# Sample rows' attention over the cached keys and values: wide instructions in place of 128-column ones, and the weighting moved to ScalarE

## The chip, the core and the metric

The kernel runs on one core of a Trainium2 chip. The metric is the device time of one execution in microseconds. In the profile PE is TensorE (matrix products), PEld its weight loads, DVE is VectorE, ACT is ScalarE, POOL is GpSimd and SP is the engine whose queue issues most DMAs.

## What is computed

One inference step of a two-layer trunk for 256 prompt tokens and 8 sample tokens at once, with a model width of 2048, in float32. Layer 0 is dilated sliding-window attention, layer 1 a state-space layer; each is followed by a gated feed-forward layer with a short convolution. The change lies in layer 0's attention of the eight sample rows:

```python
def attn_sample(h, kv_bufs, w_qkv, w_o):
    q, k, v = qkv_project(h, w_qkv, PAST_LEN + jnp.arange(S))
    for g, (win, dil) in enumerate(DIL_GROUPS):   # (128,1) (512,4) (2048,16)
        k_all = concatenate([kv_bufs[g][:, :, 0], k[:, :, g]], axis=1)
        v_all = concatenate([kv_bufs[g][:, :, 1], v[:, :, g]], axis=1)
        o, lse = dilated_attend(q[:, :, g], k_all, v_all, ...)   # 128 cached keys and the new one
    o = merge_by_denominator(outs, lses)
    return o @ w_o
```

There are 8 heads of 128 channels and 3 groups; in each head and group a sample row scores 128 cached keys, takes a softmax, and sums the 128 cached values with its weights.

## The kernel before

All activations are held with channels on the partitions and the 264 tokens on the free dimension. The weights stream in as chunks of eight 128x128 blocks, loaded by SP's queue into `wraw` (four buffers). Each chunk is split into a high part `whi` by ScalarE (line 162) and a low part `wlo` by VectorE (line 163), in three buffers each, and every block is used by three matmuls (lines 202 to 204): high by high, high by low, low by high. `gemm` walks through the blocks; at the start of each chunk it advances a counter, runs the work that `later(d, ...)` has put off by d chunks (`pump`), and loads and splits chunks up to two ahead (`ensure`). The framework orders each engine's instructions by its own plan, keeping dependences, so put-off work and splits can change places within an engine's queue; each queue then runs in order.

The query, key and value product `w_qkv` (143 chunks) goes head by head: the keys of head h, the queries of head h+1, the values of head h. In its shade runs the attention. For the prompt rows: `prompt_scores` (scores, mask, maxima on VectorE, exponentials on ScalarE, line 660) and `prompt_out` (transposes, copies, products with the values). For the sample rows and one head:

- `sample_q`: the eight queries are spread over 16 partitions each (`qx`); each partition holds eight cached keys of a group in `kc` (128 x 8 x 128). `dots` makes one dot product with an accumulated output per key on VectorE, four to a half chunk of a group (line 497), into `sc`. `sc` goes through DRAM to `ss`, with the eight rows on eight partitions.
- `sample_softmax`: maxima, exponentials and merge weights; the weighted `ss` goes through DRAM (`pd`) back to 128 partitions.
- `sample_out`: the weights come back as `pk`; for each group the eight cached values of a partition in `vc` are multiplied by their weights and added up in `ac` by VectorE (lines 619 and 621); group g one chunk after group g-1. `fin`, three chunks after the last group is begun, adds over partitions with a product by `sel` (line 625) and splits the result, the operand of the output product `w_o`.

`kc` and `vc` share six buffers (`kvc`), a head's three groups at a time. In the chunks of heads 3 to 5 VectorE and GpSimd also work, a few small steps per chunk, on the tables of the later state-space layer (`z_room`, line 912).

Of the kernel before, what the change touches and what calls it, by code (L numbers as in the profile page):

```python
"""One inference step of the dilated-attention / S5 / ConvFFN trunk on one core.

All activations are held transposed: channels on the partitions, the 264 tokens (256 prompt, 8 sample) on
the free dimension.  Weights stream through in blocks of [128 x 128] and are the stationary operand.  A
float32 product is carried by three float32r passes: each operand is split exactly into a high part H
(float32r) and the rest L, and H*H + H*L + L*H is accumulated in PSUM.
"""
# [19 lines left out]
P = 128  # L27
# [39 lines left out]
def order_grouped(mts, nk, first):  # L67
    """(k, m) blocks: the first `first` M-tiles k-outer, the others one after the other."""
    out = [(k, m) for k in range(nk) for m in mts[:first]]
    out += [(k, m) for m in mts[first:] for k in range(nk)]  # L70
    return out


def qkv_mtiles():
    """Keys of a head, the next head's queries, then the head's values."""
    seq = [(0, 0)]
    for h in range(H):
        seq += [(1, h)] + ([(0, h + 1)] if h + 1 < H else []) + [(2, h)]
    return [(which * G + g) * H + h for which, h in seq for g in range(G)]
# [24 lines left out]
class Put:  # L104
    """Notes calls to an engine for later."""
# [8 lines left out]
class Pin:  # L114
    """Calls to an engine that keep their place in its queue."""
# [8 lines left out]
class Kern:  # L124
# [12 lines left out]
    # ---------------------------------------------------------------- work put off by some chunks of weights  # L137
# [10 lines left out]
    # ---------------------------------------------------------------- helpers  # L148
# [16 lines left out]
    def ensure(self, i):  # L165
        """Load and split the weight chunks up to number i of the whole stream."""
# [13 lines left out]
    def gemm(self, name, order, nk, rhs, evac, lag=0):  # L180
        """Accumulate all blocks of `order`; rhs(k) -> (H, L) moving operands; evac(m, psum).
        The first output is taken out of PSUM `lag` chunks late, and at most two per chunk while catching up."""
# [31 lines left out]
    def ready(self, lst, k):  # L214
        """lst[k], running the put-off work until it is there."""
        while k >= len(lst) or lst[k] is None:
            self.pump()
        return lst[k]

    # ---------------------------------------------------------------- norms  # L220
    def rstd_mean(self, parts, warm=0):
        """-1/2 (mean of squares + eps) of every token, tokens on the partitions: [88, 3] in PSUM."""
# [11 lines left out]
    def rstd_root(self, mh):  # L234
        """2/3 of 1/sqrt(-2 mh): the bit-shift estimate, a step of third and a step of second order."""
# [18 lines left out]
    def rstd_spread(self, w):  # L254
        """[88, 3] -> a PSUM tile with 3/2 of every token's value on all partitions."""
# [9 lines left out]
    def warm(self, n):  # L265
        """Keeps the tensor engine's clock up over a wait: n products that nothing reads."""
# [8 lines left out]
    def rstd_soon(self, acc):  # L275
        """Puts 1/rms of the squares in acc off into the coming chunks; returns the tile that will hold it."""
# [13 lines left out]
    def squares(self, st, x):  # L290
        """st: list with the running sum of squares (made here) and the tile still to be added."""
# [10 lines left out]
    def yevac(self, ys, gi):  # L302
        """Takes a sub-layer's output out of PSUM, times the post-norm's gain; sums its squares."""
# [10 lines left out]
    def reload(self, src, wait):  # L314
        """The residual, loaded tile by tile in the coming chunks."""
# [11 lines left out]
    def operand(self, x, gi, k):  # L327
        """H/L parts of x*g (not yet scaled by 1/rms); the L part is returned as a function."""
# [10 lines left out]
    def residual(self, ys, xs, sq, keep, gi):  # L339
        """x += rms_norm(y)*g tile by tile; then the next sub-layer's operand (gain gi), its squares, the store.  # L340
        Returns rhs(k) and the tile for 1/rms."""
# [45 lines left out]
    # ---------------------------------------------------------------- constants  # L387
# [18 lines left out]
    # ---------------------------------------------------------------- attention  # L406
    def attention(self, ap, rhs, rget):
        """Returns the list that will hold the split o^T tiles, one per head."""
# [16 lines left out]
        def both(what, h, fn):  # L425
            """Runs fn when the second of its two conditions is met."""
# [48 lines left out]
    def sample_q(self, ap, st, h, g):  # L475
        """The 8 sample queries, each on 16 partitions; scores of the cached keys, 8 to a partition."""
# [17 lines left out]
        def dots(g, b0):  # L494
            for b in range(b0, b0 + 4):
                j = ap.tile([P, HD], F32, tag="junk", name=self.nm("junk"), bufs=1)
                nc.vector.tensor_tensor_reduce(  # L497
                    j, kcs[g][:, b], qx[:, g * P : (g + 1) * P], 1.0, 0.0, op0=ALU.mult, op1=ALU.add,
                    accum_out=sc[:, g, b : b + 1],
                )  # L500
            if g == G - 1 and b0:
                self.later(1, write)
# [11 lines left out]
        for g in range(G):  # L514
            self.later(1 + 2 * g, lambda g=g: dots(g, 0))
            self.later(2 + 2 * g, lambda g=g: dots(g, 4))

    def sample_new(self, ap, st, h, g):
        """Products of the sample queries with their own new keys."""
# [6 lines left out]
    def sample_softmax(self, ap, st, h):  # L526
        """Softmax weights of the sample queries over the three groups' cached and new keys."""
# [34 lines left out]
    def merge_exp(self, ap, n, tag, mg):  # L562
        """exp(SCALE*(group max - joint max)); mg is [n, groups] or [n, blocks, groups]"""
# [14 lines left out]
    def merge(self, ap, n, tag, e, l, h):  # L578
        """Merge weight of each group over head 0's sum of that group (as the reference divides)."""
# [13 lines left out]
    def sample_out(self, ap, st, h):  # L593
        """Sum of the cached and new values with the softmax weights."""
# [19 lines left out]

        def add(g):
            for e in range(8):
                w = pk[:, g, e : e + 1]
                if g == 0 and e == 0:
                    nc.vector.tensor_scalar(ac, vcs[g][:, e], w, None, op0=ALU.mult)
                else:  # L620
                    nc.vector.scalar_tensor_tensor(ac, vcs[g][:, e], w, ac, op0=ALU.mult, op1=ALU.add)  # L621
# [8 lines left out]
        for g in range(G):  # L630
            self.later(1 + g, lambda g=g: add(g))
        self.later(3 + G, fin)

    def prompt_scores(self, ap, st, h, g):
        """Masked scores of one group and their exponentials (against the group's maximum)."""
# [40 lines left out]
    def prompt_out(self, ap, st, h, os_):  # L676
        """P transposed group by group, and o^T accumulated over the groups."""
# [6 lines left out]
        def tr(g):  # L684
            # column blocks: (keys 0, queries 0), (keys 0, queries 1), (keys 1, queries 1)
# [23 lines left out]
    # ---------------------------------------------------------------- ConvFFN  # L709
    def ffn_prep(self, fp, l):  # L710
        """Convolution weights, and the part of the sample rows' convolution that the stored rows give."""
# [67 lines left out]
    # ---------------------------------------------------------------- S5  # L779
    def s5_setup(self, p):  # L780
        """What the state-space layer needs of every state: decay, phase, powers of a.  SN small steps at a time."""
# [20 lines left out]
        def exp(out, x):  # L802
            """e**x for x clamped to [-87, 88], to float32's accuracy."""
# [629 lines left out]
```

## Time and profile before

| | us |
|---|---|
| median of 3 runs (2555.21 to 2563.43) | 2557.86 |
| span of the profiled execution | 2555.1 |
| TensorE busy (matmuls) | 2469.9 |
| VectorE busy | 1817.1 |
| ScalarE busy | 1159.4 |
| GpSimd busy | 830.0 |
| attention stage beside `w_qkv`, start to the first third of `w_o` | 45 to 560 |

The time of the profiled execution is not listed apart from its span. Busy times are those in which an engine has at least one instruction running; matmuls overlap, so that a busy TensorE is not one at its peak. A windows row gives, for a stretch in us from the start of the span, its length, the busy time of each engine with the number of instructions in brackets, TensorE's granted clock as a share of 2.4 GHz, the DMA engines' busy share and GB/s.

### The profile page before, as it was taken

How to read it: one execution, taken by the hardware profiler on the slowest of the kernel's cores; microseconds unless marked ns; L12 is line 12 of the kernel's file. 1: busy time of each engine (PE TensorE's matmuls, PEld its weight loads, DVE VectorE, ACT ScalarE, POOL GpSimd, SP SyncE). 2: the span in 40 equal slices, each digit the busy share in tenths (PEclk: the TensorE clock that was granted, in tenths of full speed). 3: DMA queues.
4: the chain of work that ended last, by engine and by line, in shares of the span. 5: the costliest groups of instructions: out<-in, count | busy, mean ns of one | idle time of the engine just before them, and what ended most of it. 6: DMA issues, size and time to landing. Idle time of an engine off the chain costs nothing.

```text
span 2555.1 us, 52974 instructions
## 1 busy us (share of the span) xinstructions
PE 2469.9 (97%) x20998; PEld 2440.6 (96%) x20998; DVE 1817.1 (71%) x3490; ACT 1159.4 (45%) x1754; POOL 830.0 (32%) x1153
## 2 busy tenths in 40 slices
PE   8999999999999999999999988999999999999997
PEld 8999998999999999999999988999999999999997
DVE  6787998778988887764445878445977777764444
ACT  5344433445555555443334333444655545543332
POOL 6333347344899990011003465102100000011001
PEclk9999999999999999999999999999999999999999
DMA  7666666666666665566556677555655555566553
GB/s 274 218 234 220 210 216 203 202 213 218 202 217 217 207 217 189 182 205 199 182 181 213 212 248 240 184 181 168 198 180 179 181 181 182 182 205 200 181 182 117
DMA packets 186874, 512.14 MB, mean 200 GB/s; under 512 B 39281, under 2 KB 68993, under 8 KB 186369
## 3 DMA queue, kind: packets, MB, share of 16 engines
q1 hardware_dynamic: 141808, 457.89, 54.2%
q0 software_dynamic: 7968, 26.71, 3.3%
q10 hardware_dynamic: 36848, 24.16, 3.2%
q8 instruction: 164, 2.69, 0.4%
q14 instruction: 86, 0.70, 0.1%
HBM read 469.80 MB, written 38.88 MB: 199 GB/s over the span
## 4 chain that ended last, share of the span: by engine, by line
PE 77%; DVE 11%; issue 4%; DMA 3%; ACT 2%; POOL 1%; ACTq 1%; SPq 0%; DVEq 0%; POOLq 0%
PE ps L202 25%; PE ps L204 25%; PE ps L203 24%; DVE wlo L163 4%; DMA yb<-y 1%; DVE C L744 1%; ACT whi L162 1%; DVE ac L621 1%; DVE act L367 1%; DMA ident<-in_ident 1%; ACTq L945 0%; POOL qkv L449 0%; DMA y<-yb 0%; DVE z_room L912 0%; DVE act L335 0%
## 5 line engine op out<-in xcount | busy, mean ns | idle before, releaser
L204 PE MATMUL ps<-act,wlo 128*128 128x264 f32 x6176 | 1763.6, 286 | 30.2 <-DVE wlo L163 30.0
L202 PE MATMUL ps<-act,whi 128*128 128x264 f32 x6176 | 1771.1, 288 | 10.6 <-ACT whi L162 8.3
L203 PE MATMUL ps<-act,whi 128*128 128x264 f32 x6176 | 1760.3, 285 | 10.0 <-DVE act L335 9.8
L163 DVE TENSOR_TENSOR wlo<-wraw,whi 128x1024 fp32r<-128x1024 f32 (+1 forms) x775 | 994.2, 1283 | 555.7 <-ACT whi L162 554.6
L162 ACT ACTIVATE whi<-wraw 128x1024 fp32r<-128x1024 f32 (+1 forms) x775 | 815.9, 1055 | 1024.7 <-PE ps L203 800.5
L204 PEld LDWEIGHTS ps<-act,wlo 128*128 128x128 f32 x6176 | 1168.7, 189 | 36.9 <-DVE wlo L163 36.8
L202 PEld LDWEIGHTS ps<-act,whi 128*128 128x128 f32 x6176 | 1166.1, 189 | 16.3 <-ACT whi L162 9.1
L203 PEld LDWEIGHTS ps<-act,whi 128*128 128x128 f32 x6176 | 1169.2, 189 | 13.0 <-DVE act L335 12.2
L294 POOL TENSOR_TENSOR acc<-acc,sq 128x264 f32<-128x264 f32 x112 | 111.3, 993 | 672.8 <-ACT sq L300 670.3
L736 POOL COPY ckeep<-U 128x10 f32<-128x10 f32 x172 | 64.4, 375 | 652.5 <-DVE U L735 651.4
L744 DVE SCALAR_TENSOR_TENSOR C<-U,cw,C 128x255 f32<-128x255 f32 (+1 forms) x344 | 187.7, 547 | 0.7 <-ACT C L738 0.7
L735 DVE TENSOR_TENSOR U<-ps,rstd 128x264 f32<-128x264 f32 x172 | 73.2, 430 | 72.2 <-PE ps L204 71.8
L738 ACT ACTIVATE C<-U,cw 128x264 f32<-128x264 f32 x172 | 102.1, 596 | 17.6 <-DVE U L735 13.1
L449 POOL TENSOR_TENSOR qkv<-qkv,cs 32x264 f32<-32x264 f32 x48 | 57.3, 1194 | 148.7 <-DVE sw L443 47.4
L121 POOL TENSOR_TENSOR z_e<-z_pa,z_pb 128x256 f32<-128x256 f32 x64 | 73.1, 1142 | 5.0
L621 DVE SCALAR_TENSOR_TENSOR ac<-vc,pk,ac 128x128 f32<-128x128 f32 x184 | 69.0, 375 | 2.2
L497 DVE CUSTOM_DVE_ANT_0 junk<-kc,qx 128x128 f32<-128x128 f32 x192 | 58.4, 304 | 1.4
L660 ACT ACTIVATE S<-S,nmg 128x128 f32<-128x128 f32 (+1 forms) x48 | 21.5, 447 | 82.0 <-DVE nmg L655 82.0
L451 POOL TENSOR_TENSOR qkv<-qkv,sw 32x264 f32<-32x264 f32 x48 | 56.4, 1176 | 3.4
L121 POOL TENSOR_TENSOR z_pa<-z_bc,z_tab 128x256 f32<-128x256 f32 x64 | 55.9, 874 | 2.4
L121 POOL TENSOR_TENSOR z_pb<-z_bc,z_tab 128x256 f32<-128x256 f32 x64 | 53.6, 838 | 0.0
L749 ACT ACTIVATE C<-C 128x264 f32<-128x264 f32 x86 | 35.7, 415 | 34.1 <-DVE C L744 30.4
(213 smaller groups left out, 1698.5 us busy)
## 6 DMA issues: line engine op xcount, KB each, us to landing
wraw<-in_w_up SPq DMA_DIRECT2D x344, 512.0 KB
wraw<-in_w_down SPq DMA_DIRECT2D x172, 512.0 KB
wraw<-in_w_qkv SPq DMA_DIRECT2D x143, 512.0 KB
wraw<-in_w_glu SPq DMA_DIRECT2D x64, 512.0 KB
wraw<-in_w_in SPq DMA_DIRECT2D x32, 512.0 KB
kc<-in_kc SPq DMA_DIRECT2D x24, 512.0 KB
vc<-in_vc SPq DMA_DIRECT2D x24, 512.0 KB
wraw<-in_w_o SPq DMA_DIRECT2D x16, 512.0 KB
```

Source lines behind the costliest of these rows:

```text
L121: return lambda *a, **k: self.tc.keep_in_program_order(getattr(self.eng, name)(*a, **k))
L162: self.nc.scalar.activation(hi, src, AF.Copy)
L163: self.nc.vector.tensor_tensor(lo, src, hi.bitcast(F32), op=ALU.subtract)
L202: nc.tensor.matmul(o, hi[:, c], xh, start=first, stop=False)
L203: nc.tensor.matmul(o, hi[:, c], xl, start=False, stop=False)
L204: nc.tensor.matmul(o, lo[:, c], xh, start=False, stop=last)
L294: nc.gpsimd.tensor_tensor(st[0], st[0], st[1], op=ALU.add)
L621: nc.vector.scalar_tensor_tensor(ac, vcs[g][:, e], w, ac, op0=ALU.mult, op1=ALU.add)
L735: nc.vector.tensor_tensor(u, ps[:, 0:NT], rget(), op=ALU.mult)
L736: nc.gpsimd.tensor_copy(keep[:, m, :], u[:, NP - 2 : NT])
L738: nc.scalar.activation(c, u, AF.Identity, bias=cw[:, 3, m : m + 1], scale=cw[:, 2, m : m + 1])
L744: nc.vector.scalar_tensor_tensor(c[:, s:NP], u[:, 0 : NP - s], cw[:, j, m : m + 1], c[:, s:NP], op0=ALU.mult, op1=ALU.add)
```

## The change

The dot products of a group become two instructions on VectorE, one chunk apart: `products` multiplies the whole tile of 128x1024 by the query, repeated over the eight keys, in place; `sums` adds up the 128 channels of each of the eight keys. For the values, `weigh` multiplies the eight value blocks of a group in place by their weights on ScalarE, eight instructions of 128x128 with a per-partition scale; a chunk later `add` on VectorE adds group 1's tile, and then group 2's, to group 0's (128x1024 each), and `halve` adds the halves of that tile until 128 columns are left in `ac`. `halve` runs in the chunk of the last `add`, and `fin` is put off by one chunk more than before. The diff also empties comment lines, which leaves most lines where they were.

```diff
-        def dots(g, b0):
-            for b in range(b0, b0 + 4):
-                j = ap.tile([P, HD], F32, tag="junk", name=self.nm("junk"), bufs=1)
-                nc.vector.tensor_tensor_reduce(
-                    j, kcs[g][:, b], qx[:, g * P : (g + 1) * P], 1.0, 0.0, op0=ALU.mult, op1=ALU.add,
-                    accum_out=sc[:, g, b : b + 1],
-                )
-            if g == G - 1 and b0:
+        def products(g):
+            nc.vector.tensor_tensor(
+                kcs[g], kcs[g], qx[:, g * P : (g + 1) * P].unsqueeze(1).to_broadcast([P, 8, HD]), op=ALU.mult
+            )
+
+        def sums(g):
+            nc.vector.tensor_reduce(sc[:, g], kcs[g], axis=AX.X, op=ALU.add)
+            if g == G - 1:
                 self.later(1, write)
...
         for g in range(G):
-            self.later(1 + 2 * g, lambda g=g: dots(g, 0))
-            self.later(2 + 2 * g, lambda g=g: dots(g, 4))
+            self.later(1 + 2 * g, lambda g=g: products(g))
+            self.later(2 + 2 * g, lambda g=g: sums(g))
...
+        def weigh(g):
+            for e in range(8):
+                nc.scalar.activation(vcs[g][:, e], vcs[g][:, e], AF.Copy, scale=pk[:, g, e : e + 1])
+
         def add(g):
-            for e in range(8):
-                w = pk[:, g, e : e + 1]
-                if g == 0 and e == 0:
-                    nc.vector.tensor_scalar(ac, vcs[g][:, e], w, None, op0=ALU.mult)
-                else:
-                    nc.vector.scalar_tensor_tensor(ac, vcs[g][:, e], w, ac, op0=ALU.mult, op1=ALU.add)
+            if g:
+                self.tt(vcs[0], vcs[0], vcs[g], ALU.add)
+
+        def halve():
+            v = vcs[0]
+            self.tt(v[:, 0:4], v[:, 0:4], v[:, 4:8], ALU.add)
+            self.tt(v[:, 0:2], v[:, 0:2], v[:, 2:4], ALU.add)
+            self.tt(ac, v[:, 0], v[:, 1], ALU.add)
...
         for g in range(G):
-            self.later(1 + g, lambda g=g: add(g))
-        self.later(3 + G, fin)
+            self.later(1 + g, lambda g=g: weigh(g))
+            self.later(2 + g, lambda g=g: add(g))
+        self.later(2 + G, halve)
+        self.later(4 + G, fin)
```

## Rows read from the trace of the kernel before

**Rows 1.** The page's shares of the engines: busy us, share, instructions.
```profile
PE 2469.9 (97%) x20998; PEld 2440.6 (96%) x20998; DVE 1817.1 (71%) x3490; ACT 1159.4 (45%) x1754; POOL 830.0 (32%) x1153
```

**Rows 2.** Windows of the attention stage, columns PE, PEld, DVE, ACT, POOL, clock, DMA.
```profile
75.00:100.00 25.00, 23.19 (x186) 22.37 (x184) 24.38 (x117) 11.90 (x24) 4.11 (x7) 1.00 0.70 232
120.00:150.00 30.00, 25.60 (x179) 24.62 (x180) 28.94 (x92) 12.48 (x30) 13.06 (x16) 0.89 0.61 198
260.00:280.00 20.00, 17.89 (x146) 17.46 (x145) 19.61 (x70) 9.38 (x21) 8.28 (x9) 1.00 0.46 143
315.00:420.00 105.00, 95.63 (x748) 92.60 (x747) 103.36 (x352) 41.28 (x79) 57.25 (x70) 0.99 0.60 201
280.00:315.00 35.00, 35.00 (x282) 34.56 (x281) 33.13 (x134) 13.19 (x22) 11.37 (x13) 1.00 0.74 257
160.00:260.00 100.00, 99.94 (x804) 98.09 (x803) 79.81 (x268) 41.62 (x76) 39.42 (x44) 1.00 0.68 230
500.00:510.00 10.00, 8.08 (x52) 7.78 (x51) 6.81 (x16) 2.88 (x6) 6.39 (x7) 0.83 0.29 83
45.00:560.00 515.00, 493.06 (x3881) 481.34 (x3880) 441.94 (x1457) 211.49 (x396) 230.30 (x276) 0.99 0.65 216
```

**Rows 3.** Waits in 45:560: who for whom, us in total, times, longest.
```profile
ACT whi L162 <- PE ps L203: 164.5, 78, 5.7
...
PE ps L204 <- DVE wlo L163: 20.8, 17, 2.7
```

**Rows 4.** VectorE's groups by line in 45:560: busy us, mean ns, idle before.
```profile
L163 DVE TENSOR_TENSOR wlo<-wraw,whi 128x1024 fp32r<-128x1024 f32 x144 | 188.2, 1308 | 26.3 <-ACT whi L162 25.6 <-PE ps L688 0.2
L621 DVE SCALAR_TENSOR_TENSOR ac<-vc,pk,ac 128x128 f32<-128x128 f32 x184 | 69.0, 375 | 2.2
L497 DVE CUSTOM_DVE_ANT_0 junk<-kc,qx 128x128 f32<-128x128 f32 x192 | 58.4, 304 | 1.4
L437 DVE TENSOR_TENSOR qkv<-ps,rstd 128x264 f32<-128x264 f32 x72 | 30.2, 423 | 1.8 <-PE ps L204 1.7
...
L497 DVE DVE_READ_ACCUMULATOR2_ANT sc<- 128x1 f32 x192 | 15.5, 81 | 0.0
...
L536 DVE TENSOR_REDUCE mgs<-ss 8x3 f32<-8x384 f32 x8 | 4.3, 540 | 29.0 <-DMA ss<-sd 29.0
...
L619 DVE TENSOR_SCALAR ac<-vc,pk 128x128 f32<-128x128 f32 x8 | 3.3, 412 | 4.0 <-DMA pk<-pd 4.0
...
L613 DVE TENSOR_REDUCE of<-vn 128x8 f32<-128x24 f32 x8 | 1.4, 175 | 0.0
```

**Rows 5.** VectorE in order of time, 100:180: start us, length us.
```profile
130.59 1.76 DVE L163 TENSOR_TENSOR wlo<-wraw,whi 128x1024 fp32r<-128x1024 f32 x1
```

**Rows 6.** Windows of the multiply-add line L621 in the saturated stretches, summed.
```profile
sum 180.00, DVE 28.97; mean DVE 7.24
```

**Rows 7.** The same of the dot-product line L497.
```profile
sum 180.00, DVE 22.14; mean DVE 5.53
```

**Rows 8.** ScalarE in order of time, 20:40 and 120:123.
```profile
31.43 0.91 ACT L332 ACTIVATE act<-xa,gn 128x264 fp32r<-128x264 f32 x2
...
121.05 0.40 ACT L660 ACTIVATE S<-S,nmg 128x128 f32<-128x128 f32 x1 [2.74 <-DVE nmg L655]
121.36 0.19 ACT L660 ACTIVATION_READ_ACCUMULATOR S<-S,nmg 128x1 f32 x1
```

**Rows 9.** The chain of waits in 541:543: start us, length us, what.
```profile
542.11 0.22 PE ps L695 x2
542.33 0.12 PE ps L625 x2
```

**Rows 10.** Waits of SP's DMA queue in 45:560.
```profile
SPq L604 <- DVE ac L621: 4.8, 3, 2.3
```

## The prediction

> **What bounds the kernel now.** I read the shares of the engines first [rows 1]. TensorE is busy 2469.9 of 2555.1 us: over the whole program the matmuls are the limit. That is an average over stages. The change touches only the attention stage, the stretch from 45 to 560 us. Its windows [rows 2] give TensorE 493.06 of 515 us, VectorE 441.94 (86%) and ScalarE 211.49 (41%). So TensorE stands idle 21.9 us in the stage that the change touches, and this, with a few microseconds of lowered clock, is all that a lighter VectorE can win back.
>
> Next, who makes TensorE wait: in this stage nearly always `wlo`, the low part of a weight chunk, which VectorE computes [rows 3]. The windows show where VectorE is the reason [rows 2]. In 75:100, 120:150, 260:280 and 315:420 VectorE is busy 24.38 of 25, 28.94 of 30, 19.61 of 20 and 103.36 of 105 us, together 176.3 of 180 (98%), and TensorE is idle 1.8, 4.4, 2.1 and 9.4 us, 17.7 in sum. The granted clock is 0.89 over 30 us and 0.99 over 105: parts of these stretches, behind idle times of TensorE, ran at the lower of the two levels (1.2 instead of 2.4 GHz), which costs about 0.11 x 30 + 0.01 x 105 = 4.4 us. **The budget is thus 22 us** where VectorE is saturated. In 160:260 VectorE is busy 80% and TensorE idles 0.06 us; in 280:315 it is 95% and 0. So a small relief is enough, if it comes evenly. The stretch 500:510, with 1.9 us idle and a clock of 0.83 (1.7 us more), is another case: VectorE is busy only 6.81 of 10 there.
>
> **The change part by part.** The VectorE groups of the stage [rows 4] price what goes. Scores: 192 dot products of 128 columns (58.4 us) and their 192 accumulator reads (15.5), 73.9 us. Values: 184 multiply-adds (69.0) and 8 first products (3.3), 72.3 us.
>
> What comes on VectorE. The 24 products of 128x1024 are two-input instructions of the size of `wlo`, 1308 ns mean [rows 4]: 31 us. That one operand repeats the query over eight keys no row shows; below I bound it by nothing, above by the stretched `wlo` of 1.76 us [rows 5], 11 us more in all, and I take nothing, since both operands are still read one element for one. The 24 sums of 1024 columns have no row either. The nearest reductions are 128x24 in 175 ns and 8x384 in 540 ns [rows 4], so 365 ns for 360 more elements, 1.01 ns each; 1024 come to 0.54 + 640 x 0.00101 = 1.19 us, 28.6 us in all. The slope alone, 1.04 us, is the lower bound; two passes, 2.4 us, the upper. I take 1.19. Scores are then 60 us, 14 less than now. The Trainium skill, page "VectorE: DVE Perf Modes", section "Rules for kernel authors", speaks against this half: it calls the reduction the slowest VectorE operation and advises restructuring around it. By our two rows the scores win 14 us all the same; with sums at the upper bound they would lose 15, and that is a rival below.
>
> Values on VectorE, per head: two additions of 1024 columns (2 x 1.3), then 512, 256 and 128. Between the 264-column product (423 ns) and the 1024-column one (1308) an element costs 1.16 ns, so 0.71, 0.41 and 0.27 us; 4.0 us a head, 32 us for eight, 40 less than now. **Together VectorE loses about 54 us of 442.** The four saturated stretches hold 29.0 us of the value line and 22.1 of the score line [rows 6, 7]; at 32/72 and 60/74 of that they lose 16 + 4 = 20 us, and 176 of 180 become 156, 87%, between the loads of 160:260 and 280:315, which show no idle TensorE.
>
> What comes on ScalarE: 192 weightings of 128 columns with a per-partition scale. No such row; the 264-column ones with a per-partition gain go two in 0.91 us [rows 8], so 0.455 each is the upper bound. A 128-column exponential, with a per-partition bias, is followed 0.31 us later by its accumulator read [rows 8], and I take that, being the same width, also as the lower bound. So 2.5 us for a group's eight and 60 us in all (to 87). ScalarE goes from 211 to 271 of 515 us, 53%: not a bound. The Trainium skill, page "ScalarE: Activation LUTs", section "Rules for kernel authors", would keep multiplications on VectorE. Left there as single products at 412 ns [rows 4], the weightings would cost VectorE 79 us, more than is saved, and nothing would be won; at 0.31 us on ScalarE the rows side with the move.
>
> What hides ScalarE's 60 us is its own waiting: it waits 164.5 us in 78 times for TensorE to free a `whi` buffer [rows 3], 2.1 us each, and TensorE wants a chunk two chunks later, 2 x 24 x 0.124 = 6.0 us (35 us for 282 matmuls in 280:315), of which 1.05 for `whi` and 1.3 for `wlo` go off. So a delay of 2.1 + 3.6 = 5.7 us costs nothing, and a burst of 2.5 fits. But the first weighting also takes over VectorE's wait for the reloaded weights (`pk`), now 4.0 us over all heads [rows 4]. Behind it on ScalarE stand the next `whi`, for which `wlo` and then TensorE wait, the prompt rows' exponentials and the copies of transposed values. A ScalarE that comes to `pk` earlier than VectorE did waits longer there. I put 3 us of idle TensorE on this, between 0 and 29 (below).
>
> Parts priced at nothing. The value tile of group 0 is held until the last halving, four chunks longer, the others one chunk longer. SP's queue, with the weight loads in it, waits for these buffers: the next value load now waits 4.8 us for the multiply-adds [rows 10]. The cover is that weights are loaded up to four chunks ahead; without it these microseconds would count, at most 5. The final step comes one chunk later. For seven heads nobody waits for it. For the last head TensorE takes the sample product at 542.33 us straight behind the prompt's last product [rows 9], so the prompt side ends as late. ScalarE's 24 weightings (7.5 us) from about 528 us, three `whi` among them, an addition and the halvings (2.7) end near 541: 0, at most 2 us. The later stages get the same work.
>
> **The sum.** Of 22 us I take two thirds, 15, since the relief is uneven: 75:100 has no value work and loses only the scores' part, while its TensorE idles 1.8 us like the others. Less 3 on ScalarE: 12 us. The profiled execution's time is not listed apart from its span, 2555.1 us, which is 2.8 under the median of the three runs, 2557.86. Against the span the sum is 2543; with the 2.8 for a median **2546 us**, with a range of its own of 2539 to 2550.
>
> **The rivals.** *All of the stall goes*, and the loss at 500:510 with it as that stretch is re-timed: 22 + 3.6 = 26 us, 2532. For it: 280:315 idles nothing at 95%. Against: the losses are single late chunks, and instructions of 1.3 us can stand before a `wlo` as four short ones did. Chance 0.12.
>
> *VectorE's relief is not turned into time*, 2551 to 2562. VectorE waits 29.0 us for the scores' reload and 25.6 us for `whi` [rows 4]; where a late chunk comes from these, less work on VectorE moves nothing, and a later ScalarE gives the rest back. Against: the four stretches hold only 3.7 us of idle VectorE in all. If the sums take 2.4 us, which is the way in which the change would not do what it says, VectorE loses only 25 us, the time is near 2553 and falls in here too. Chance 0.29.
>
> *Slower:* ScalarE stands at `pk` in front of `whi`. From a wait of 5.7 - 2.5 = 3.2 us on, the chunk is late; VectorE's wait was 0.5 us a head on average, so ScalarE must get there some 3 us before VectorE would have. The price is that of the event at 500:510, 1.9 us idle and 1.7 of clock; eight heads make 29 us, and with the 15 won before, 2558 - 15 + 29 = 2572; from four heads on the gain is eaten. For it: ScalarE is the less loaded engine and so the earlier one. Chance 0.15.
>
> **How the numbers follow.** Forecast 0.44, all gone 0.12, no change 0.29, slower 0.15. 0.3% is 7.7 us, about what a measurement of this kernel can tell; the forecast's own range lies below 2550.2, so faster 0.56, same 0.29, slower 0.15. The range goes down to 2532, where all is gone, and up to 2564, which leaves out most of the case with eight late heads; a tenth is left out on each side.
>
> **What would show it.** Right: VectorE in 45:560 at about 390 us, products near 1.3 and sums near 1.2 us, weightings 0.31 us apart, TensorE's waits for `wlo` in the stage under 10 us, the clock at 1.00 around 140 us. Wrong: a ScalarE wait for `pk` above 3 us with a late `whi` behind it; `wlo` waits as many as before with VectorE idle in front of them; sums beyond 2 us.

## The result, and the profile after

The changed kernel takes 2545.43 us, median of four runs (2542.86 to 2546.09), beside 2558.37 us (2555.21 to 2563.43), now of four runs, for the kernel before on the same chip: a ratio of 0.9943, 95% interval 0.9929 to 0.9957. That is 12.9 us less, where 12 were forecast (2546). The range, 2532 to 2564, holds it, and "faster by over 0.3%" came true. The split of these microseconds is not the predicted one, and most of what follows is about that.

The profiled execution of the changed kernel took 2546.09 us, its span 2544.3, 10.8 less than the span before. The page's shares, to be held against [rows 1]:

```profile
PE 2466.5 (97%) x20998; PEld 2440.0 (96%) x20998; DVE 1800.9 (71%) x3002; ACT 1214.1 (48%) x1946; POOL 851.6 (33%) x1153
```

VectorE lost only 16.2 us of busy time, ScalarE gained 54.7, GpSimd 21.6 with the same number of instructions. The windows of the attention stage, beside [rows 2] (columns PE, PEld, DVE, ACT, POOL, clock, DMA; the same work lies up to 14 us earlier here at the stage's end):

```profile
75.00:100.00 25.00, 22.85 (x186) 22.30 (x185) 25.00 (x50) 11.18 (x23) 6.89 (x7) 1.00 0.79 248
120.00:150.00 30.00, 27.70 (x210) 27.08 (x211) 27.48 (x77) 19.61 (x55) 17.71 (x17) 0.94 0.61 202
260.00:280.00 20.00, 19.68 (x163) 19.47 (x162) 19.69 (x53) 14.70 (x33) 4.41 (x6) 1.00 0.65 200
315.00:420.00 105.00, 99.49 (x774) 97.56 (x774) 99.59 (x254) 55.77 (x127) 59.15 (x71) 0.97 0.65 212
500.00:510.00 10.00, 10.00 (x83) 9.62 (x82) 7.28 (x33) 5.76 (x17) 2.31 (x5) 1.00 0.70 229
45.00:560.00 515.00, 502.59 (x3995) 493.30 (x3995) 435.17 (x979) 271.59 (x597) 259.40 (x282) 0.99 0.66 221
```

TensorE's idle time in 75:100, 120:150, 260:280 and 315:420 falls from 17.7 to 10.3 us. VectorE is still busy 171.8 of 180 us there, after 176.3. The clock is 0.94 in 120:150, where it was 0.89, but 0.97 in 315:420, where it was 0.99: 5.0 us are lost to the lower level (1.2 GHz) in these stretches, as before (4.4). In 500:510 TensorE idles no more, nor anywhere from 470 us to the end of the stage. The waits of the stage, beside [rows 3, 4]:

```profile
DVE wlo L163 <- ACT whi L162: 49.4, 38, 7.1
...
ACT vc L617 <- DMA pk<-pd: 18.4, 8, 5.5
...
PE ps L204 <- DVE wlo L163: 9.4, 8, 2.4
...
DVE mgs L536 <- DMA ss<-sd: 7.9, 3, 4.1
...
PE ps L481 <- POOL qe L454: 1.9, 1, 1.9
```

TensorE's waits for `wlo` fall from 20.8 us in 17 to 9.4 in 8. VectorE stands 7.9 us before the reloaded scores (`ss`) instead of 29.0, and the stand at `pk`, 4.0 us on VectorE before, has become 18.4 on ScalarE. VectorE's groups in the stage, beside [rows 4] (busy us, mean ns, idle before):

```profile
L163 DVE TENSOR_TENSOR wlo<-wraw,whi 128x1024 fp32r<-128x1024 f32 x149 | 196.7, 1321 | 49.6 <-ACT whi L162 49.4
L495 DVE TENSOR_TENSOR kc<-kc,qx 128x1024 f32<-128x1024 f32 x24 | 30.4, 1279 | 0.0
...
L500 DVE TENSOR_REDUCE sc<-kc 128x8 f32<-128x1024 f32 x24 | 28.9, 1206 | 0.0
...
L153 DVE TENSOR_TENSOR vc<-vc,vc 128x1024 f32<-128x1024 f32 x16 | 19.6, 1225 | 0.6 <-ACT vc L617 0.6
...
L153 DVE TENSOR_TENSOR vc<-vc 128x512 f32<-128x512 f32 (+1 forms) x16 | 10.1, 630 | 0.2
...
L153 DVE TENSOR_TENSOR ac<-vc 128x128 f32<-128x128 f32 x8 | 5.2, 656 | 0.1
...
L536 DVE TENSOR_REDUCE mgs<-ss 8x3 f32<-8x384 f32 x8 | 4.3, 535 | 7.9 <-DMA ss<-sd 7.9
```

The stage is best measured up to its first matmul of line 272, which follows the last product of `w_o`: at 576.5 us before and 562.4 after. Of the 531.5 and 517.4 us from 45 on, TensorE is idle 21.9 and 12.4; the granted clock is at its lower level for 13.6 and 10.2 us of the trace, which costs half of that. So of the 14.1 us that the stage got shorter, 9.5 are idle time, 1.7 are clock, and 2.9 are neither. Most of the 2.9 are short delays that do not show as idle time: products of lines 202 to 204 start 0.12 us apart and their records last 0.28, so that TensorE counts as busy through a small delay. Where such a distance, idle time left out, is above 0.15 us at the upper clock, the excess over 0.12 adds up to 15.6 us before and 13.1 after. The later stages, with the same instructions, came out 3.3 us longer (1978.6 and 1981.9 us of span); in the profiled executions of all fourteen kernels below they lie between 1978.6 and 1982.8, so a difference of 4 us between two executions can come from behind the stage, and this part is not the change's.

### The profile page after: what moved, and what is told of

Its sections match the earlier page's. It is cut to its first block, busy times and chain, and to the rows that moved or that the text cites. A ratio compares the mean times of both kernels' runs of the same rounds, so it can differ in the third digit from the quotient of the medians.

```text
span 2544.3 us, 52668 instructions
## 1 busy us (share of the span) xinstructions
PE 2466.5 (97%) x20998; PEld 2440.0 (96%) x20998; DVE 1800.9 (71%) x3002; ACT 1214.1 (48%) x1946; POOL 851.6 (33%) x1153
## 4 chain that ended last, share of the span: by engine, by line
PE 73%; DVE 12%; issue 4%; DMA 4%; POOL 3%; ACT 3%; ACTq 1%; SPq 0%; DVEq 0%; POOLq 0%
PE ps L202 24%; PE ps L203 23%; PE ps L204 23%; DVE wlo L163 4%; DMA yb<-y 1%; DVE C L752 1%; ACT whi L162 1%; POOL z_room L920 1%; DVE z_room L920 1%; DVE act L367 1%; DMA y<-yb 1%; DMA ident<-in_ident 1%; ACTq L953 1%; DVE act L335 1%; POOL qkv L449 0%
## 5 line engine op out<-in xcount | busy, mean ns | idle before, releaser
L204 PEld LDWEIGHTS ps<-act,wlo 128*128 128x128 f32 x6176 | 1168.2, 189 | 22.9 <-DVE wlo L163 22.8
L617 ACT ACTIVATE vc<-vc,pk 128x128 f32<-128x128 f32 x192 | 59.4, 389 | 18.4 <-DMA pk<-pd 18.4
L768 DVE TENSOR_TENSOR act<-C,act 128x264 fp32r<-128x264 f32 x86 | 49.8, 579 | 0.5 <-ACT act L766 0.5
L450 POOL TENSOR_TENSOR sw<-sw,cs 32x264 f32<-32x264 f32 x48 | 49.5, 1032 | 0.0
```

The source lines that it names most:

```text
L204: nc.tensor.matmul(o, lo[:, c], xh, start=False, stop=last)
```

## The experiments

They were made in three sessions on different chips, each beside the kernel before, whose median was 2559.19 us (`a` to `d`), 2557.99 (`e`, `g`, `h`, `i`) and 2558.97 (`j` to `m`). The theories that the expectations speak of: the gain comes from VectorE's load (L); from the time in which VectorE is held, its busy time and its stands at the two reloads together (H); from steps that come at other times, above all the maxima behind the scores' reload (R); ScalarE's bursts of weightings, placed where they are, cost part of it (S); any shift in the planned order moves the stage by some microseconds (P).

The table has, for the stage from 45 us to the first matmul of line 272 in each profiled execution: its length, TensorE's idle time, busy times, and VectorE's stands at `ss` and at `pk` (where ScalarE weights the values, the stand at `pk` is ScalarE's).

| kernel | median us | ratio, interval | stage us | TensorE idle | VectorE busy | ScalarE busy | stand at `ss`, `pk` |
|---|---|---|---|---|---|---|---|
| before | 2558.37 | | 531.5 | 21.9 | 452.1 | 218.5 | 29.0, 4.0 |
| changed | 2545.43 | 0.9943 (0.9929-0.9957) | 517.4 | 12.4 | 436.8 | 272.5 | 7.9, ScalarE 18.4 |
| a_scores | 2549.41 | 0.9965 (0.9952-0.9977) | 521.0 | 15.5 | 467.4 | 218.7 | 2.5, 2.3 |
| b_values | 2546.83 | 0.9958 (0.9944-0.9971) | 519.3 | 15.5 | 427.8 | 271.3 | 24.0, ScalarE 16.9 |
| c_weigh_dve | 2558.77 | 1.0004 (0.9995-1.0012) | 531.3 | 24.0 | 474.5 | 218.8 | 3.2, 3.0 |
| d_late_softmax | 2561.43 | 1.0007 (0.9997-1.0018) | 533.8 | 21.8 | 452.1 | 218.5 | 16.9, 13.5 |
| l_late_softmax7 | 2552.98 | 0.9980 (0.9969-0.9990) | 527.2 | 16.9 | 454.0 | 219.0 | 14.4, 8.6 |
| g_values_late | 2554.06 | 0.9984 (0.9975-0.9993) | 527.0 | 20.5 | 427.1 | 271.6 | 21.7, ScalarE 16.2 |
| h_sums_twice | 2564.27 | 1.0024 (1.0014-1.0034) | 537.6 | 25.6 | 458.4 | 272.2 | 9.7, ScalarE 18.8 |
| i_weigh_twice | 2559.00 | 1.0004 (0.9995-1.0013) | 532.1 | 22.8 | 433.8 | 338.4 | 10.2, ScalarE 16.3 |
| e_late_weigh | 2538.64 | 0.9924 (0.9910-0.9938) | 512.4 | 9.8 | 433.4 | 273.2 | 5.8, ScalarE 16.8 |
| j_late_last | 2541.25 | 0.9927 (0.9914-0.9939) | 515.6 | 12.0 | 435.4 | 272.7 | 6.3, ScalarE 18.2 |
| k_later_weigh | 2542.49 | 0.9932 (0.9918-0.9945) | 516.1 | 12.1 | 432.6 | 272.8 | 5.2, ScalarE 18.0 |
| m_split_weigh | 2539.57 | 0.9922 (0.9908-0.9935) | 515.1 | 13.2 | 433.0 | 272.7 | 6.8, ScalarE 16.6 |

**One half each.** `a_scores` is the kernel before with `products` and `sums` alone, `b_values` with `weigh`, `add` and `halve` alone.

Against the changed kernel, `a` takes back the values' steps and `b` the scores', with the functions of before:

```diff
-            self.later(1 + g, lambda g=g: weigh(g))
-            self.later(2 + g, lambda g=g: add(g))
-        self.later(2 + G, halve)
-        self.later(4 + G, fin)
+            self.later(1 + g, lambda g=g: add(g))
+        self.later(3 + G, fin)
```

```diff
-            self.later(1 + 2 * g, lambda g=g: products(g))
-            self.later(2 + 2 * g, lambda g=g: sums(g))
+            self.later(1 + 2 * g, lambda g=g: dots(g, 0))
+            self.later(2 + 2 * g, lambda g=g: dots(g, 4))
```

> The scores' half of the change alone: products and sums on VectorE, the values as before. Theory L (load): the gain of 12 us comes from a lighter VectorE; the time in which the score line runs went only from 60.0 us (union of its instructions) to 59.3, so this half gives 0 to 3 us, and VectorE's time in the stage falls by under 5. Theory R (re-timing): the gain comes from VectorE no longer standing at the maxima for the scores' reload (29.0 us before, 7.9 after); the sums are done sooner, so this half gives 7 us or more and that wait falls below 12.

> The values' half alone: weights on ScalarE, additions on VectorE, the dot products as before. Theory L: 9 to 12 us gained, VectorE's value lines from 72 to 35 us. Theory R: 0 to 4 us gained, and the maxima still wait some 25 us for the scores' reload.

Both halves win, 9.8 and 12.4 us against that session's 2559.19, and together no more than 12.9: they draw in part on the same idle time of TensorE. Of its idle times above 0.8 us in the kernel before, those that end at 132.41, 265.59, 273.18, 339.65 and 504.41 us (6.4 us together) are in neither half. How they win differs: for `a_scores` R's expectation came true and L's did not, for `b_values` it was the other way round (L had 9 to 12 us). With the scores' half alone VectorE is *more* busy than before (467.4 for 452.1 us), but it stands 2.5 us at the scores' reload instead of 29.0. With the values' half alone VectorE loses 24.3 us of busy time and keeps most of its stand (24.0).

**The weightings on VectorE.** `c_weigh_dve` is the changed kernel with them there.

```diff
-                nc.scalar.activation(vcs[g][:, e], vcs[g][:, e], AF.Copy, scale=pk[:, g, e : e + 1])
+                nc.vector.tensor_scalar(vcs[g][:, e], vcs[g][:, e], pk[:, g, e : e + 1], None, op0=ALU.mult)
```

> The changed kernel with the 192 weightings on VectorE (0.2 to 0.3 us each, 38 to 54 us) in place of ScalarE. Theory L: VectorE is as loaded as before or more, so the gain is gone: 2556 to 2566 us, and the waits for the low weight part are back at 20 us or more. Theory R: at least half of the gain stays, below 2552.

The whole gain is gone: 1.0004. VectorE goes up 37.7 us from the changed kernel, to 474.5, and TensorE's idle time with it, from 12.4 to 24.0. The stand at the reload is small here (3.2), so a small stand alone wins nothing; the load counts. But L expected 20 us or more of waits for `wlo`, and not all of the loss is there:

```profile
PE ps L204 <- DVE wlo L163: 15.3, 15, 2.5
...
PE ps L647 <- POOL qkv L451: 5.3, 2, 3.0
```

The second row, 0.4 us in the changed kernel, is a wait for GpSimd, and why GpSimd comes later here is not shown. The move to ScalarE is what the values' half lives on, against the rule of the Trainium skill (page "ScalarE: Activation LUTs", section "Rules for kernel authors") that multiplications belong on VectorE, for which it names the speed per element in bf16: in this stage, in float32 and with a loaded VectorE, the measurement decides for ScalarE.

**More load on either engine.** `h_sums_twice` makes every sum of the changed kernel twice, `i_weigh_twice` every weighting, the first time into a tile that nothing reads.

```diff
+            nc.vector.tensor_reduce(sc[:, g], kcs[g], axis=AX.X, op=ALU.add)
             nc.vector.tensor_reduce(sc[:, g], kcs[g], axis=AX.X, op=ALU.add)
```

```diff
+                j = ap.tile([P, HD], F32, tag="junk", name=self.nm("junk"), bufs=1)
+                nc.scalar.activation(j, vcs[g][:, e], AF.Copy, scale=pk[:, g, e : e + 1])
                 nc.scalar.activation(vcs[g][:, e], vcs[g][:, e], AF.Copy, scale=pk[:, g, e : e + 1])
```

> The changed kernel with each of the 24 sums done twice, 29 us more VectorE work at 1.2 us each. Theories H and L: held time 1838 instead of 1809, so at least 5 us of the gain go: 2550 to 2556. Rival (plan): it is the fewer, better foreseen instructions that bring the gain, not the time that they take; then at most 3 us are lost, under 2549.

> The changed kernel with each of the 192 weightings done twice, the first into a tile that nobody reads: 60 us more on ScalarE. Theory H: ScalarE has the room (267 of 505 us busy in the stage, and it waits 125 us for TensorE), so at most 3 us are lost, under 2549. Rival S: ScalarE already delays the high parts (VectorE's wait for them went from 25.6 to 45.5 us); then it loses 5 us or more, above 2551.

Twenty-four more sums, 21.6 us more busy time on VectorE, cost 18.8 us against the changed kernel: nearly one for one, and some 8 us beyond the range that H and L gave. Sixty-six more microseconds on ScalarE cost 13.6, far above H's 3. That is the time that S expected, but not by its way: VectorE's wait for `whi` is 51.0 us in the stage, after 50.7. More than half of the 13.6 is one place, the last head, where no other work covers the weightings. The windows of that run (columns as above):

```profile
535.00:540.00 5.00, 4.23 (x35) 4.01 (x33) 1.28 (x2) 4.77 (x15) 0.00 (x0) 1.00 0.44 161
540.00:545.00 5.00, 0.88 (x4) 0.79 (x5) 2.96 (x6) 0.98 (x4) 0.00 (x0) 0.88 0.00 0
545.00:550.00 5.00, 4.99 (x23) 4.68 (x22) 2.34 (x4) 3.13 (x7) 3.10 (x4) 0.50 0.01 3
```

TensorE is idle 4.9 us in 535:545, with 4.4 of it a wait for `ac`, and then runs for 6.8 us at the lower clock, 3.4 more: 8.3 of the 13.6. The other 5 us or so arose in the seven heads before; what held them up is not shown.

**The maxima later.** `d_late_softmax` and `l_late_softmax7` are the kernel before with `sample_softmax` two chunks later, in all heads or in all but the last; `g_values_late` is the values' half with it in all heads. The edit of `d` and `g`, and that of `l`:

```diff
-            self.later(2, lambda: self.both("softmax", h, self.sample_softmax))
+            self.later(4, lambda: self.both("softmax", h, self.sample_softmax))
```

```diff
-            self.later(2, lambda: self.both("softmax", h, self.sample_softmax))
+            self.later(4 if h < H - 1 else 2, lambda: self.both("softmax", h, self.sample_softmax))
```

> The kernel before, its sample softmax put off by two more chunks after the reload is issued, so that VectorE does not stand at the maxima. Theory R: that wait falls from 29 us to under 10 and 5 to 10 us are gained. Theory L: the wait falls as well, but VectorE's load is the same and the time stays within 3 us of before.

> The values' half alone, with the sample softmax put off by two more chunks. Theory H (held time): what counts is the time in which VectorE cannot do a low weight part, its busy time plus the time in which it stands at the head of its queue for the scores' reload or the weights' reload: 1850 us before, 1809 in the changed kernel, 1836 with the scores' half, 1816 with the values' half. Here the stand for the scores' reload, 24.0 us in the values' half, falls below 10, held time goes to about 1800, and 2 to 5 us are gained on the values' half, so that it comes to the changed kernel or below, 2541 to 2546 us. Theory L (busy time alone): busy time is that of the values' half, so the time stays within 2 us of it, 2545 to 2549.

> The kernel before with the maxima two chunks later for heads 0 to 6 only, the last head as before, so that nothing is added behind the last head. Theory R (VectorE's stand at the scores' reload is what the change gave back by moving steps): the stand at the reload falls from 29 to below 20 us and the time by 4 us or more, to 2554 or less. Theory L (VectorE's load alone counts): its load is unchanged, so within 3 us of the kernel before.

In `d` nothing was won, and the stand at `ss` fell only to 16.9 us, where R had it under 10. But its last head was late: TensorE waited 3.4 us for `ac` at the stage's end, and 6.8 us at the lower clock followed. `l` was made to leave that out. It takes 6.0 us less than the kernel before, as R had it, with VectorE's busy time unchanged (454.0 for 452.1) and its stands shorter (14.4 for 29.0 at `ss`, 8.6 for 4.0 at `pk`); its waits and windows:

```profile
DVE mgs L536 <- DMA ss<-sd: 14.4, 5, 4.1
PE ps L204 <- DVE wlo L163: 13.1, 14, 1.8
```

```profile
500.00:510.00 10.00, 10.00 (x83) 9.95 (x82) 7.70 (x21) 4.25 (x12) 4.53 (x6) 1.00 0.55 163
45.00:572.20 527.20, 510.26 (x4016) 499.56 (x4015) 454.02 (x1469) 218.96 (x406) 237.84 (x283) 0.98 0.66 217
```

So time can be won with the load unchanged, and L alone does not explain the gain. That it was the shorter stand that won all of the 6.0 us is not shown: the edit moves other steps too. For one stand the kernel before shows how it is paid, in VectorE's order of time, and in TensorE's:

```profile
492.82 1.21 DVE L163 TENSOR_TENSOR wlo<-wraw,whi 128x1024 fp32r<-128x1024 f32 x1
501.89 0.54 DVE L536 TENSOR_REDUCE mgs<-ss 8x3 f32<-8x384 f32 x1 [7.86 <-DMA ss<-sd]
...
503.15 2.34 DVE L163 TENSOR_TENSOR wlo<-wraw,whi 128x1024 fp32r<-128x1024 f32 x2
```

```profile
504.41 0.39 PE L204 MATMUL ps<-act,wlo 128*128 128x264 f32 x1 [1.92 <-DVE wlo L163]
```

VectorE stands 7.86 us at `ss`, with the next low parts queued behind the maxima; when it comes to them, TensorE has been waiting 1.92 us. In `l` and in the changed kernel TensorE is busy 10.00 of these 10 us. `g` speaks against reading too much into the stand: its stand fell only from 24.0 to 21.7, and it is 7 us slower than `b_values`, where H had it 2 to 5 us faster and L within 2 us, with waits of TensorE for GpSimd's `qe` (5.4 us) and for other small operands that `b_values` does not have.

**The weightings later.** `e_late_weigh` is the changed kernel with `weigh`, `add`, `halve` and `fin` one chunk later; `k_later_weigh` two chunks; `m_split_weigh` is `e` with the eight weightings in two bursts of four half a chunk apart; `j_late_last` moves only `fin` (the halvings, which its expectation counts to the moved step, stay). The edits of `e`, of `m` against `e` (with `weigh` taking four blocks from `e0` on), and of `j`; `k` puts one more chunk on each line of `e`:

```diff
-            self.later(1 + g, lambda g=g: weigh(g))
-            self.later(2 + g, lambda g=g: add(g))
-        self.later(2 + G, halve)
-        self.later(4 + G, fin)
+            self.later(2 + g, lambda g=g: weigh(g))
+            self.later(3 + g, lambda g=g: add(g))
+        self.later(3 + G, halve)
+        self.later(5 + G, fin)
```

```diff
-            self.later(2 + g, lambda g=g: weigh(g))
+            self.later(2 + g, lambda g=g: weigh(g, 0))
+            self.later(2.5 + g, lambda g=g: weigh(g, 4))
```

```diff
-        self.later(4 + G, fin)
+        self.later(5 + G, fin)
```

> The changed kernel with weightings, additions and the last step one chunk later, so that ScalarE comes to the reloaded weights later than now (its wait there is 18.4 us over the eight heads). Rival S: that wait falls below 8 us and 3 us or more are gained, under 2543. Theory H: VectorE is not held by it, the time stays within 2 us of the changed kernel.

> The changed kernel with only each head's last sample-row step (halve, divide, write back) one chunk later. Theory S (the ScalarE burst in front of the PSUM exponentials is what the order of steps sets): nothing that ScalarE waits for has moved, so within 2.5 us of the changed kernel's 2545. Theory P (any shuffle of the planned order moves the sample-row stage by chance): 3 to 6 us either way, below 2542 or above 2548.

> The changed kernel with weightings, sums, halvings and the last step two chunks later than planned, one more than in the run with one. Theory S: the wait of ScalarE for the probabilities' reload falls clearly below 16 us and the time is no more than that run's 2538.6, some 2535 to 2540. Theory P: no trend, anything from 2535 to 2552, the wait unchanged.

> The run with the weightings one chunk later, each group's eight weightings now in two bursts of four, half a chunk apart. Theory S (bursts of 2.4 us on ScalarE hold up the exponentials that TensorE's tiles wait for): 1 to 3 us better than 2538.6, below 2538. If a burst of eight fits in the slack of the ring of exponentials: within 2 us of that run, 2537 to 2541.

`e` came out 6.8 us under the changed kernel, 4.9 by the ratios, which looked like S. The other three do not bear that out. `j`, in which nothing that ScalarE weights has moved, is 4.2 us under the changed kernel as well; `k`, later still, is no better than `e`; splitting the bursts changes 0.9 us. ScalarE's wait for `pk` stays between 16.6 and 18.4 us in all five, where S had it under 8 in `e`. So S falls. The intervals of the four overlap one another and that of the changed kernel, so it is not shown that any of them is faster than the changed kernel. P is not shown either: the profiled span of `j` is 4.8 us shorter than the changed kernel's, but its stage only 1.8, and the other 3.0 lie behind the stage, where the instructions are the same. `e`, at 2538.64 us, has the lowest median; all four beat the kernel before.

## Why the prediction was right, and where its terms were not

That the number came out within a microsecond is partly luck: one term was too large by more than three times, and a saving that was not forecast made up for it.

**The bound and the wait** held: TensorE's waits for `wlo` are what moved, to under 10 us, as forecast (9.4).

**Prices of what comes** held. Products 1279 ns (1.3 us forecast), so repeating the query over eight keys costs nothing that shows. Sums 1206 ns (1.19). Values on VectorE 34.9 us (32). Weightings follow each other every 0.30 us (0.31), and ScalarE came to 272.5 us in the stage (271). For the weightings the forecast had taken a distance from start to start; by their recorded length of 389 ns they would have come to 75 us. That nothing is won with them on VectorE held as well (`c`), though they run for 52 us there and not the 79 of the forecast.

**The failed step is "Together VectorE loses about 54 us of 442".** It lost 15.3 in the stage. What went was priced by adding durations of instructions that overlap. VectorE in order of time in the kernel before shows it (start us, length us):

```profile
156.47 0.28 DVE L497 CUSTOM_DVE_ANT_0 junk<-kc,qx 128x128 f32<-128x128 f32 x1
156.68 0.08 DVE L497 DVE_READ_ACCUMULATOR2_ANT sc<- 128x1 f32 x1
156.68 0.35 DVE L621 SCALAR_TENSOR_TENSOR ac<-vc,pk,ac 128x128 f32<-128x128 f32 x1
156.95 0.28 DVE L497 CUSTOM_DVE_ANT_0 junk<-kc,qx 128x128 f32<-128x128 f32 x1
157.16 0.08 DVE L497 DVE_READ_ACCUMULATOR2_ANT sc<- 128x1 f32 x1
157.16 0.35 DVE L621 SCALAR_TENSOR_TENSOR ac<-vc,pk,ac 128x128 f32<-128x128 f32 x1
157.42 0.29 DVE L497 CUSTOM_DVE_ANT_0 junk<-kc,qx 128x128 f32<-128x128 f32 x1
...
531.23 1.90 DVE L621 SCALAR_TENSOR_TENSOR ac<-vc,pk,ac 128x128 f32<-128x128 f32 x5
```

The accumulator read and the next multiply-add start together, before the dot product's recorded end, and here a pair of dot product and multiply-add goes every 0.48 us, where the sum of the three means is 0.76. Only 53 of the 184 multiply-adds are followed at once by a dot product; the others overlap in the same way with other instructions of VectorE. Over the whole stage VectorE has an instruction of the two lines running for 122.8 us, not 146.2, and for 97.3 of these it runs nothing else. In the changed kernel the instructions that replace them run for 94.2 us, 83.3 of them with nothing else. These 14.0 us are nearly all of the 15.3. The line of the dot products alone, as a window of the kernel before (length, busy):

```profile
45.00:576.00 531.00, 60.01 (x384) 0.99 0.65 216
```

Dots and their reads thus hold VectorE 60.0 us, not 73.9, and the two wide instructions that replace them 59.3. The scores' half relieves VectorE of nothing, where the forecast had 14 us. The Trainium skill's warning (page "VectorE: DVE Perf Modes", section "Rules for kernel authors") that the reduction is the slowest operation and worth restructuring around fits that there was no saving, but its ground does not show here: a sum of 1024 columns took 1206 ns and a product of the same size 1279, and `a_scores` was 9.8 us faster. In `a_scores` VectorE is busier than before because the two lines run for 138.1 us there, after 122.8: dot products no longer lie under multiply-adds, and the value line itself takes 79.0 us, after 72.3.

**"Of 22 us I take two thirds, 15"** was nearly right as a sum and wrong as to the place. The four saturated stretches gave 7.4 us of idle time and no clock, half of what was taken, as VectorE is still 95% busy in them (forecast 87%). The stretch 500:510, which the forecast set aside as another case, gave all of its 3.6 us. It was the stand of 7.86 us at the scores' reload. The reload is not in the change; it was listed among the rivals as a reason against a gain ("where a late chunk comes from these, less work on VectorE moves nothing"), and this stretch and `l` show it as a source of one. So a smaller relief of load and a shorter stand, which was not forecast, add up to what one large relief was to bring. How much each gave can't be split: L and R both win when tested alone, `c` shows that the short stand wins nothing when the load is high, and the sum of VectorE's busy time and its stands (H) puts seven kernels in an order that the times bear out as far as they can be told apart (before 485 us, `d` 482 and `c` 481, these three with like times; `l` 477, `a` 472, `b` 452, the changed kernel 445; the four with later steps follow with 438 to 442), but not `g`, `h` and `i` (449, 468 and 444). What made `g` 7 us slower than `b` stays open too.

**"Less 3 on ScalarE", for its wait at `pk`.** The wait became longer than the condition of the slower rival: 4.26, 5.51 and 3.75 us in three heads, where 3.2 was to be the point from which a chunk comes late. Nothing came late behind them. ScalarE and TensorE in order of time, changed kernel:

```profile
385.21 1.99 ACT L162 ACTIVATE whi<-wraw 128x1024 fp32r<-128x1024 f32 x2
392.71 1.57 ACT L617 ACTIVATE vc<-vc,pk 128x128 f32<-128x128 f32 x5 [5.51 <-DMA pk<-pd]
394.20 1.04 ACT L162 ACTIVATE whi<-wraw 128x1024 fp32r<-128x1024 f32 x1
```

```profile
387.72 0.39 PE L204 MATMUL ps<-act,wlo 128*128 128x264 f32 x1 [2.44 <-DVE wlo L163]
...
412.19 0.39 PE L204 MATMUL ps<-act,wlo 128*128 128x264 f32 x1 [0.83 <-DVE wlo L163]
```

From 387.2 to 394.20 us ScalarE splits no weights, 7.0 us with the five weightings, and TensorE's next stall is at 411.4. The stall of 2.44 us ends at 387.72, half a microsecond into the wait: it is older. VectorE shows what stood in front of that `wlo`:

```profile
385.29 0.15 DVE L590 TENSOR_TENSOR me<-me,z 8x3 f32<-8x3 f32 x1
385.47 0.99 DVE L550 TENSOR_TENSOR ss<-ss,me 8x384 f32<-8x384 f32 x1
386.39 0.14 DVE L551 TENSOR_TENSOR sn<-sn,me 8x3 f32<-8x3 f32 x1
386.46 1.21 DVE L163 TENSOR_TENSOR wlo<-wraw,whi 128x1024 fp32r<-128x1024 f32 x1
```

By count this is the 112th `wlo`. Its `whi`, the 112th, is the second of these rows of ScalarE:

```profile
381.93 0.40 ACT L668 ACTIVATE S<-S,nmg 128x128 f32<-128x128 f32 x1 [3.44 <-DVE nmg L663]
...
383.68 1.04 ACT L162 ACTIVATE whi<-wraw 128x1024 fp32r<-128x1024 f32 x1
```

ScalarE stood 3.44 us for the prompt rows' maxima, made two sets of exponentials, and split the chunk from 383.68 to 384.72. Then the `wlo` stood 1.7 us on VectorE behind the sample rows' softmax, small instructions that follow from one another, and a product of 8x384 that takes 0.99 us here. The stall at 323.28 (2.22 us) has the same history, with a stand of 3.56 us on ScalarE. A third one, at 138.94 (2.02 us), has steps of the sample rows' softmax and a 1024-column addition of 1.20 us in front of its `wlo`. These three are 6.7 of the 9.4 us that are left.

**Two of its signs failed.** VectorE in 45:560 is busy 435 us, not 390, which is the failed step again. The clock around 140 us did not stay at 1.00: TensorE ran at the lower level from 140.0 to 143.5 us, behind the idle time of 2.02 us that ended at 138.94.

**Parts priced at nothing** show nothing: in the changed kernel no wait of TensorE for `ac` or `sel`'s product is among those of the last head, and ScalarE's waits for weight loads fell from 13.0 to 5.7 us in the stage. The value buffers' longer hold was not tried by itself.

**The rivals.** All of the stall going (2532) did not come; of all kernels `e` has the least idle time, 9.8 us. No change (2551 to 2562) is what `c` measures, so this rival describes the kernel without the move to ScalarE. The slower one had its condition met in three heads and its price not paid.

## What to carry to other kernels

Before adding up the durations of instructions that a change removes, look at their starts in order of time: where they overlap, the start-to-start distance is the price, and it depends on what stands between them. An engine that stands at a late transfer can cost the engine behind it time as one that computes does (here 7.86 us of standing cost 3.6), so look at its stands beside its load. Try steps a chunk later, and measure: the same shift came with 6 us less in one kernel (`l`) and 7 us more in another (`g`). Where a planner orders the queues, put one control run that shifts an unrelated step beside an experiment on order: here such a run (`j`) lay 4 us off, as much as the effect that was looked for.

## What the runs showed of the hardware

The same addition of 128 columns takes 0.29 us or 0.83 us. VectorE in the changed kernel:

```profile
363.39 0.83 DVE L153 TENSOR_TENSOR ac<-vc 128x128 f32<-128x128 f32 x1
...
527.70 0.29 DVE L153 TENSOR_TENSOR ac<-vc 128x128 f32<-128x128 f32 x1
```

Of the eight such additions two took 0.26 and 0.29 us and six 0.72 to 0.84; in 0.7 us from the start of each of the six GpSimd was busy 0.62 to 0.70 us, and at 527.70 not at all. Wider additions do not always show it: a 1024-column one at 291.72 us took 1.20 us with GpSimd busy throughout (all sixteen took 1203 to 1346 ns), and of two 256-column ones with GpSimd busy throughout one took 0.40 us (421.39) and one 0.87 (230.54). The Trainium skill (page "GPSIMD Engine Reference", section "1. Specifications") names contention of the two engines on shared SBUF interfaces for VectorE instructions with two inputs there; the 128-column rows agree with it, and what decides in the wider ones is not shown. Multiply-adds into the same `ac`, each using the result of the one before, follow every 0.38 us where nothing stands between them (the five in 1.90 us at 531.23, shown above), but one between two dot products is followed after 0.27 us (156.68 to 156.95). In the attention stage the lower clock came for 3.4 or 6.8 us, within or right behind an idle time of TensorE, but not with each: in the kernel before one followed the 1.92 us at 504.41 and none the 1.85 us at 329.22, in `l` one followed 1.41 us at 333.18.
